# One addition moved from a DMA to VectorE, and single PSUM tiles at three places of a two-layer trunk

## The chip, the cores and the metric

The kernel runs on one core of one Trainium2 chip. The metric is the device time of one execution in microseconds, as the median of several. Before the change it is 2025.73 us, the median of three runs (2024.69 to 2026.8).

## What is computed

A trunk of two layers on x, 256 tokens by 2048 features, in float32. Layer 0 mixes by causal pooling, layer 1 by dilated attention over one shared K and V; each is followed by a norm, a gated FFN with a causal convolution of width 3, and another norm. Cut to what matters here:

```python
for i in range(DEPTH):                      # DEPTH = 2
    if i < N_A_LAYERS:                      # layer 0: w_in, pooling over 2/4/8/16 tokens, w_grp, w_out
        mix = pool_mixer(h, ...)
    else:                                   # layer 1: 16 heads of 128, three dilated windows merged
        mix = dilated_attention(h, k_shared, v_shared, w_q, w_o)
    h = layer_norm(DEEPNORM_ALPHA * h + mix, ln1_g[i], ln1_b[i])
    ff = conv_ffn(h, w_up, conv_w, conv_b, w_down)      # (silu(gate) * val) @ w_down
    h = layer_norm(DEEPNORM_ALPHA * h + ff, ln2_g[i], ln2_b[i])
```

## The kernel before

**Split products.** TensorE multiplies in a format that rounds float32. So each matrix is split into a high part (`wh`, `xc` high) and the rest (`wl`, `xc` low), and three products make one. ScalarE casts the high part, VectorE subtracts it for the low part: L99 and L100 for weights, L553 and L554 for x. Weights go through in *units* of 512 rows by 512 columns (1 MB). `run_units` works through a list of units in a fixed order: loads run up to five units ahead, splits up to three, and `later(n, fn)` puts a step n units on. `before[i]` holds steps for the start of unit i. Each engine's queue has the order in which this program writes its instructions; nothing is reordered.

**Activations.** The stream stands feature by feature in four quarters of 512 features, `H[0]` to `H[3]`, each 128 partitions by 4 blocks by 256 tokens. `XC[q]` is its split copy. At the start `x_quad(q)` turns a quarter of x by eight transposes (L548) into PSUM, casts and subtracts two halves of it into `XC[q]`, and later copies it into `H[q]` (L557). Quarters 1 to 3 are turned in the middle of units 0 to 2; a unit's first eight steps (blocks k = 0 and 1) lie ahead of them, the rest behind.

**PSUM.** One pool has four slots of two banks. `pair` takes a slot, and `bank` takes a slot too but uses only its first bank. The framework that places the waits goes by tile: a reader waits for all writers of a tile that stand ahead of it, and readers of one tile on two engines wait for each other. A new tile in a slot waits until the old one is read.

**Norms.** The residual of a group of four blocks is added to its quarter by VectorE (`resid_last`, L338 and L340). After quarter 0, its mean over features is made by a product with ones and turned round (`cs`, `shift`), and taken from all four quarters, so that the sums of squares stay small. The pooling layer and the attention do that with VectorE. In the first FFN (`first` is false) quarter 0 is done by VectorE (L394), and quarters 1 to 3 by DMAs from POOL's queue that add in place (`less`, L409). Then `stats` and `folds` gather sums S and squares Q over the quarters, and `chain` makes two products with ones of them (L429 and L430), behind the unit that follows the last quarter.

**The last two heads.** `outputs(3, (2, 3))` multiplies the weights of the attention with V for two heads into one PSUM tile (L1114, L1115), casts and subtracts each into `oq[3]` (L1119, L1120). It stands right ahead of the unit that reads them, the last of the first group of `attn_w_o`.

**The final norm.** `finish1` ends the second half of the tokens. Three quarters get b minus the mean times g from TensorE (L940 and L947), and VectorE multiplies the stream in from PSUM (L952, L955) ahead of the stores.

Of the kernel before, what the change touches and what calls it, by code (L numbers as in the profile page):

```python
# [9 lines left out]
F32 = mybir.dt.float32  # L10
# [3 lines left out]
OP = mybir.AluOpType  # L14
# [3 lines left out]
T = 256  # L18
P = 128
# [13 lines left out]
def trunk(ctx: ExitStack, tc: tile.TileContext, x, pool_w_in, pool_w_grp, pool_scale, pool_w_out,  # L33
# [3 lines left out]
    V, A, PE = nc.vector, nc.scalar, nc.tensor  # L37
# [10 lines left out]
    def pair(nm):  # L48
        return psp.tile([P, 2, 512], F32, name=nm, tag="ps")

    def bank(nm):
        return pair(nm)[:, 0, :]
# [19 lines left out]
    pending, before = [], {}  # L72
# [62 lines left out]
    def later(n, fn):  # L135
        if n == 0:
            fn()
        else:
            pending.append([n, fn])
# [158 lines left out]
    def w4(nm):  # L298
        return lnp.tile([P, 4, T], F32, name=nm, tag="w4")

    def quad_tile(nm):
        return xcp.tile([P, 4, 2, XW], F32R, name=nm, tag="xc")
# [12 lines left out]
    H, XC, XP, ST = {}, {}, {}, {}  # L315
    vec, cvec, gbx = [], [], {}
    ident = const.tile([P, P], F32, name="ident")
# [39 lines left out]
    def square(q, m):  # L357
        if m == 0:
            ST["sq"] = lnp.tile([P, 4, T], F32, name="sq", tag="sq")
        A.activation(ST["sq"][:, m:m + 2], H[q][:, m:m + 2], AF.Square)  # L360
# [12 lines left out]
    def folds(q):  # L373
        ST["S"] = fold(H[q], ST["S"], "S")
        ST["Q"] = fold(ST["sq"], ST["Q"], "Q")

    def stats(q):
        square(q, 0)
        square(q, 2)
        folds(q)  # L380

    def shift(s, first, lay, which):
        ps = bank("shift")
        PE.matmul(ps[:, :T], ones4, s, start=True, stop=True)
        if first:
            cs = ST["w4"][:, 3:4, :]
        else:
            cs = pools["ffn"].tile([P, 2, T], F32, name="cs", tag="xs", bufs=1)[:, 0:1, :]
        A.activation(cs[:, 0, :], ps[:, :T], AF.Copy, scale=-1.0)
        cb = cs.to_broadcast([P, 4, T])  # L390
        ST["S"] = ST["Q"] = None

        def one():
            V.tensor_tensor(H[0], H[0], cb, OP.add)  # L394
            if first:
                pre(1)
            stats(0)

        def two():
            xp(0, lay, which)  # L400
            if first:
                pre(2)
                pre(3)

        def pre(q):
            V.scalar_tensor_tensor(H[q], H[q], ALPHA, cb, op0=OP.mult, op1=OP.add)

        def less(q):
            nc.gpsimd.dma_start(H[q], cb, accum_op=OP.add)  # L409

        later(1, one)
        later(2, two)
        if not first:
            for q in (1, 2, 3):
                less(q)

    def xp(q, lay, which):
# [118 lines left out]
    def x_quad(q, halves=(0, 1)):  # L536
        xin = XIN
        if halves[0] == 0:
            H[q] = hp.tile([P, 4, T], F32, name="h", tag="h")
            XC[q] = quad_tile("xc")  # L540
        if halves[0] == 0:
            ST["xT"] = pair("xT")
        both = ST["xT"]
        for half in halves:
            for kk in range(2):
                for t in range(2):
                    k = 2 * half + kk
                    PE.transpose(both[:, half, kk * T + t * P:kk * T + t * P + P], xin[q, t][:, k * P:(k + 1) * P],  # L548
                                 ident)
        for half in halves:  # L550
            pv2 = both[:, half, :].rearrange("p (k t) -> p k t", k=2)
            s = slice(2 * half, 2 * half + 2)
            A.copy(XC[q][:, s, 0, :T], pv2)  # L553
            V.tensor_tensor(XC[q][:, s, 1, :T], pv2, XC[q][:, s, 0, :T].bitcast(F32), OP.subtract)  # L554
        if halves[-1] == 1:
            before.setdefault(min(q + 1, 3), []).append(
                lambda: A.copy(H[q], both.rearrange("p b (k t) -> p (b k) t", k=2)))  # L557

    def add_in(g, mids=()):
        group(pool_w_in[0], rows4, 512 * g, 512, xsrcs, pool_post(g), mode="a" if g == 3 else "ab", mids=mids)  # L560
# [3 lines left out]

    marks = []
    add_in(3, mids=[lambda q=q: x_quad(q) for q in (1, 2, 3)])
    add_in(2)
    add_grp(3)
# [295 lines left out]
    def tm_post(lay, n, c):  # L864
        parts = [slice(0, 256), slice(256, 512)]
        first, last = n == 0, n == 3
# [66 lines left out]
        def finish1():  # L933
            mv = lnp.tile([P, 6], F32, name="mv", tag="mv", bufs=2)
            V.bn_aggr(mv[:, 0:2], ST["bn"][:, 1])
            z = [HT[cc][:, 1, :] for cc in range(4)]
            g, b = [ST["g"][:, cc, :] for cc in range(4)], [ST["b"][:, cc, :] for cc in range(4)]
            ps = [p[:, i, :] for p in (pair("gb"), pair("gb")) for i in range(2)]
            for cc in range(3):
                PE.matmul(ps[cc], ident, b[cc], start=True, stop=False)  # L940
            A.activation(mv[:, 2:3], mv[:, 1:2], AF.Sqrt, bias=epst)
            V.reciprocal(mv[:, 3:4], mv[:, 2:3])
            V.scalar_tensor_tensor(mv[:, 4:5], mv[:, 0:1], -1.0, mv[:, 3:4], op0=OP.mult, op1=OP.mult)
            dg = w4("dg")[:, 0, :P]
            V.tensor_scalar(dg, ident, mv[:, 4:5], None, op0=OP.mult)
            for cc in range(3):
                PE.matmul(ps[cc], dg, g[cc], start=False, stop=True)  # L947
            V.scalar_tensor_tensor(z[3], z[3], mv[:, 0:1], g[3], op0=OP.subtract, op1=OP.mult)
            V.scalar_tensor_tensor(z[3], z[3], mv[:, 3:4], b[3], op0=OP.mult, op1=OP.add)
            store(nc.scalar, 3, 1)  # L950
            for cc in range(2):
                V.scalar_tensor_tensor(z[cc], z[cc], mv[:, 3:4], ps[cc], op0=OP.mult, op1=OP.add)  # L952
                store((nc.sync, nc.scalar)[cc], cc, 1)
            for by, c in zip((nc.sync, nc.scalar), parts):
                V.scalar_tensor_tensor(z[2][:, c], z[2][:, c], mv[:, 3:4], ps[2][:, c], op0=OP.mult, op1=OP.add)  # L955
                store(by, 2, 1, c)
# [7 lines left out]
    qk, pr, oq, pT, vts = {}, {}, {}, {}, {}  # L964
# [140 lines left out]
    def outputs(hq, ms):  # L1105
        if ms[0] == 0:
            oq[hq] = quad_tile("o")
        vt = vts[hq]
        both = pair("o")
        for m in ms:  # L1110
            hd = slice(m * P, (m + 1) * P)
            ps = both[:, m % 2, :]
            t = pT.pop((hq, m))
            PE.matmul(ps[:, :T], vt[:, 0, hd], t[:, :T], start=True, stop=False)  # L1114
            PE.matmul(ps[:, P:T], vt[:, 1, hd], t[:, T:], start=False, stop=True)  # L1115
        o = oq[hq][:, ms[0]:ms[0] + 2]
        for at in (slice(0, 1), slice(1, 2)) if hq == 3 else (slice(0, 2),):
            hi = o[:, at, 0, :T]
            A.copy(hi, both[:, at, :T])  # L1119
            V.tensor_tensor(o[:, at, 1, :T], both[:, at, :T], hi.bitcast(F32), OP.subtract)  # L1120

    def v_group(hq):
        js = (0, 1, 2, 3)
# [18 lines left out]
    with tc.tile_pool(name="start", bufs=1) as stp:  # L1142
        one1 = stp.tile([P, P], F32, name="one1")
        for q in range(NQ):
            for t in range(2):
                XIN[q, t] = stp.tile([P, 512], F32, name=f"xin{q}{t}")
            halves = [slice(0, 256), slice(256, 512)] if q == 0 else [slice(0, 512)]
# [130 lines left out]
```

## Time and profile before

| what | value |
|---|---|
| median of three runs | 2025.73 us |
| the profiled execution | 2024.98 us |
| its span | 2023.2 us |
| TensorE busy (share of the span) | 2011.6 us (99%) |
| VectorE busy | 1728.5 us (85%) |
| ScalarE busy | 1269.2 us (63%) |
| POOL busy | 94.3 us (5%) |
| granted TensorE clock over the span | 0.999 |
| mean DMA rate | 202 GB/s |

The span is what the profile sees of the execution; the rest of the 2024.98 us lies around it. TensorE's busy time counts overlapping products once, so a stop shows in the waits and in the timeline rather than in this share.

### The profile page before, as it was taken

The numbers are of one execution on the slowest core, as the hardware profiler recorded it, in microseconds if no ns is written. First come the engines' busy times: TensorE is split into PE (matmuls) and PEld (weight loads), VectorE is DVE, ScalarE is ACT, GpSimd is POOL, SyncE is SP. The second block draws the span as 40 slices with busy tenths as digits, with TensorE's granted clock in tenths as the row PEclk, the third lists the DMA queues.
The fourth block names the chain that finished last, engine by engine and source line by source line (L and its number), as shares of the span: only waits on it lengthen the run. The fifth ranks groups of instructions, "written<-read, shape, count | busy, mean of one in ns | idle before, by whom it ended". The sixth has DMA issues, their size and how long they took to land.

```text
span 2023.2 us, 31428 instructions
## 1 busy us (share of the span) xinstructions
PE 2011.6 (99%) x12742; PEld 1813.7 (90%) x12742; DVE 1728.5 (85%) x1822; ACT 1269.2 (63%) x1546; POOL 94.3 (5%) x154
## 2 busy tenths in 40 slices
PE   9999999999999999999999999999999999999999
PEld 8898988999899988888898988998899989989987
DVE  6868887999899999779796878787899899989898
ACT  5454686766766676656554444477767677667672
POOL 2000000000000000000000021000000000000000
PEclk9999999999999999999999999999999999999999
DMA  8565576676666767885565656557666757666765
GB/s 256 192 211 188 164 216 191 180 221 222 197 198 205 233 190 219 236 226 187 177 207 165 199 175 207 188 175 221 167 215 203 227 179 227 193 222 189 211 220 173
DMA packets 271825, 408.30 MB, mean 202 GB/s; under 512 B 74446, under 2 KB 86116, under 8 KB 271424
## 3 DMA queue, kind: packets, MB, share of 16 engines
q1 hardware_dynamic: 259488, 388.93, 59.1%
q0 software_dynamic: 11760, 16.70, 5.5%
q8 instruction: 100, 1.64, 0.3%
q10 hardware_dynamic: 432, 0.66, 0.1%
q14 instruction: 45, 0.37, 0.1%
HBM read 380.01 MB, written 2.10 MB: 189 GB/s over the span
## 4 chain that ended last, share of the span: by engine, by line
PE 98%; DVE 1%; DMA 0%; issue 0%; ACT 0%; SPq 0%; DVEq 0%
PE acc L180 44%; PE acc L181 22%; PE s L246 3%; PE s L244 3%; PE s L245 3%; PE acc L185 3%; PE t L246 2%; PE t L244 2%; PE t L245 2%; PE acc L184 2%; PE acc L183 2%; PE t L255 2%; PE t L257 2%; PE t L256 2%; PE s L1064 0%; PE o L1114 0%
## 5 line engine op out<-in xcount | busy, mean ns | idle before, releaser
L180 PE MATMUL acc<-xc,wh 128*128 128x512 f32 x3264 | 1151.8, 396 | 0.0
L181 PE MATMUL acc<-xc,wl 128*128 128x256 f32 x3264 | 916.0, 281 | 0.0
L100 DVE TENSOR_TENSOR wl<-raw,wh 128x2048 fp32r<-128x2048 f32 (+2 forms) x305 | 657.1, 2163 | 174.9 <-ACT wh L99 170.3
L180 PEld LDWEIGHTS acc<-xc,wh 128*128 128x128 f32 x3264 | 616.0, 189 | 143.3
L99 ACT CAST wh<-raw 128x2048 fp32r<-128x2048 f32 (+2 forms) x305 | 548.7, 1805 | 170.1 <-PE acc L180 70.4
L181 PEld LDWEIGHTS acc<-xc,wl 128*128 128x128 f32 x3264 | 615.4, 189 | 0.1
L113 ACT CAST wh<-raw 128x1024 fp32r<-128x1024 f32 x142 | 148.4, 1052 | 194.5 <-DVE raw L122 175.3
L114 DVE TENSOR_TENSOR wl<-raw,wh 128x1024 fp32r<-128x1024 f32 x142 | 169.4, 1221 | 11.2 <-ACT wh L113 11.2
L121 DVE TENSOR_TENSOR wl<-raw,wh 128x1536 fp32r<-128x1536 f32 x71 | 124.5, 1754 | 6.7 <-ACT wh L119 5.7
L119 ACT CAST wh<-raw 128x1536 fp32r<-128x1536 f32 x71 | 104.9, 1477 | 35.4 <-PE acc L180 28.2
L287 POOL DMA_DIRECT2D ht<-w x48 | 41.3, 1014 | 1446.7 <-DVE ht L877 722.1
L246 PE MATMUL t<-wh,g 128*128 128x256 f32 x376 | 105.7, 281 | 0.0
L244 PE MATMUL t<-wh,g 128*128 128x256 f32 x376 | 105.6, 281 | 0.0
L245 PE MATMUL t<-wl,g 128*128 128x256 f32 x376 | 105.4, 280 | 0.0
L620 ACT ACTIVATE c<-u,cv 128x256 f32<-128x256 f32 x172 | 89.5, 592 | 23.1 <-DVE f L682 16.6
L246 PE MATMUL s<-wh,xs 128*128 128x256 f32 x344 | 96.2, 280 | 0.0
L244 PE MATMUL s<-wh,xs 128*128 128x256 f32 x344 | 96.1, 279 | 0.0
L245 PE MATMUL s<-wl,xs 128*128 128x256 f32 x344 | 96.0, 279 | 0.0
L124 DVE TENSOR_TENSOR raw<-raw 128x1024 f32<-128x1024 f32 x71 | 87.0, 1225 | 2.4
L625 ACT ACTIVATE a<-u,cv 128x256 f32<-128x256 f32 x172 | 73.4, 499 | 11.9 <-DVE g L692 11.9
L611 ACT COPY u<-acc 128x512 f32<-128x512 f32 x84 | 46.9, 573 | 47.4 <-PE acc L181 47.1
L625 ACT ACTIVATE u<-u,cv 128x256 f32<-128x256 f32 x172 | 73.4, 499 | 0.0
(337 smaller groups left out, 3445.2 us busy)
## 6 DMA issues: line engine op xcount, KB each, us to landing
raw<-in_ffn_w_up_dram SPq DMA_DIRECT2D x160, 1024.0 KB, 5.2
raw<-in_ffn_w_down_dram SPq DMA_DIRECT2D x80, 1024.0 KB, 5.2
raw<-in_pool_w_out_dram SPq DMA_DIRECT2D x16, 1024.0 KB, 5.0
raw<-in_shared_w_k_dram SPq DMA_DIRECT2D x16, 1024.0 KB, 5.1
raw<-in_attn_w_q_dram SPq DMA_DIRECT2D x16, 1024.0 KB, 5.1
raw<-in_shared_w_v_dram SPq DMA_DIRECT2D x16, 1024.0 KB, 5.2
raw<-in_attn_w_o_dram SPq DMA_DIRECT2D x16, 1024.0 KB, 5.4
ht<-w POOLq DMA_DIRECT2D x50, 256.0 KB, 5.3
```

What stands on the lines that cost most here:

```text
L99: A.copy(wh[i][:, s], r[:, s])
L100: V.tensor_tensor(wl[i][:, s], r[:, s], wh[i][:, s].bitcast(F32), OP.subtract)
L113: A.copy(h[:, :, n], r[:, :, n])
L114: V.tensor_tensor(l[:, :, n], r[:, :, n], h[:, :, n].bitcast(F32), OP.subtract)
L119: A.copy(hs, rs)
L121: V.tensor_tensor(ls, rs, hs.bitcast(F32), OP.subtract)
L180: PE.matmul(ps[m].ap, h[:, k, c], q[:, k, :, :T], start=st, stop=False)
L181: PE.matmul(ps[m][:, :T], l[:, k, c], q[:, k, 0, :T], start=False, stop=sp)
L244: PE.matmul(to, xh, h[:, k, n], start=opens and kk == 0, stop=False)
L245: PE.matmul(to, xh, l[:, k, n], start=False, stop=False)
L246: PE.matmul(to, xl, h[:, k, n], start=False, stop=ends and kk == 1)
L625: A.activation(to[:, m, :], u[:, m, i:i + T], AF.Copy, scale=cv[:, i, j:j + 1])
```

## The change

Four edits.

1. In the first FFN the mean is added to quarter 1 by VectorE, right behind quarter 0, in the step `one`. Only quarters 2 and 3 are left to the DMAs.
2. `x_quad` takes a PSUM tile for each half of a quarter. The four transposes of a half are followed by its cast and its subtraction, then the next half's come. The copy into `H[q]` is made half by half, at the start of unit q instead of unit q + 1 (unit 3 for the last two quarters).
3. The last two heads get a PSUM tile each, and each head is cast and subtracted behind its own products. Heads 0 and 1 of that group are cast as one again.
4. The final norm's three products get a PSUM tile each instead of two tiles for pairs.

```diff
@@ shift, one()
             V.tensor_tensor(H[0], H[0], cb, OP.add)
             if first:
                 pre(1)
+            else:
+                V.tensor_tensor(H[1], H[1], cb, OP.add)
             stats(0)
...
         if not first:
-            for q in (1, 2, 3):
+            for q in (2, 3):
                 less(q)
@@ x_quad
-        if halves[0] == 0:
-            ST["xT"] = pair("xT")
-        both = ST["xT"]
         for half in halves:
+            ps = bank("xT")
             for kk in range(2):
                 for t in range(2):
                     k = 2 * half + kk
-                    PE.transpose(both[:, half, kk * T + t * P:kk * T + t * P + P], xin[q, t][:, k * P:(k + 1) * P],
-                                 ident)
-        for half in halves:
-            pv2 = both[:, half, :].rearrange("p (k t) -> p k t", k=2)
+                    PE.transpose(ps[:, kk * T + t * P:kk * T + t * P + P], xin[q, t][:, k * P:(k + 1) * P], ident)
+            pv2 = ps.rearrange("p (k t) -> p k t", k=2)
             s = slice(2 * half, 2 * half + 2)
             A.copy(XC[q][:, s, 0, :T], pv2)
             V.tensor_tensor(XC[q][:, s, 1, :T], pv2, XC[q][:, s, 0, :T].bitcast(F32), OP.subtract)
-        if halves[-1] == 1:
-            before.setdefault(min(q + 1, 3), []).append(
-                lambda: A.copy(H[q], both.rearrange("p b (k t) -> p (b k) t", k=2)))
+            before.setdefault(q, []).append(lambda s=s, pv2=pv2: A.copy(H[q][:, s, :], pv2))
@@ finish1
-            ps = [p[:, i, :] for p in (pair("gb"), pair("gb")) for i in range(2)]
+            ps = [bank("gb") for cc in range(3)]
@@ outputs
-        both = pair("o")
+        last = hq == 3 and ms[0] == 2
+        both = None if last else pair("o")
         for m in ms:
             hd = slice(m * P, (m + 1) * P)
-            ps = both[:, m % 2, :]
+            ps = bank("o") if last else both[:, m % 2, :]
...
+            if last:
+                hi = oq[hq][:, m, 0, :T]
+                A.copy(hi, ps[:, :T])
+                V.tensor_tensor(oq[hq][:, m, 1, :T], ps[:, :T], hi.bitcast(F32), OP.subtract)
-        o = oq[hq][:, ms[0]:ms[0] + 2]
-        for at in (slice(0, 1), slice(1, 2)) if hq == 3 else (slice(0, 2),):
-            hi = o[:, at, 0, :T]
-            A.copy(hi, both[:, at, :T])
-            V.tensor_tensor(o[:, at, 1, :T], both[:, at, :T], hi.bitcast(F32), OP.subtract)
+        if not last:
+            o = oq[hq][:, ms[0]:ms[0] + 2]
+            A.copy(o[:, :, 0, :T], both[:, :, :T])
+            V.tensor_tensor(o[:, :, 1, :T], both[:, :, :T], o[:, :, 0, :T].bitcast(F32), OP.subtract)
```

How the instructions stand on VectorE in the first FFN's norm, before. Each row has the line, the operation, what is written and read, and the size; `h_7393` is quarter 0 and `h_7713` quarter 1 of the stream, `cs` the mean turned round.

```order
L394 TENSOR_TENSOR h_7393<-h_7393,cs_8470 128x1024
L364 TENSOR_TENSOR fold_8426<-h_7393 128x512
L367 TENSOR_TENSOR S_8510<-fold_8426 128x256
L364 TENSOR_TENSOR fold_8426<-sq_8506 128x512
L367 TENSOR_TENSOR Q_8513<-fold_8426 128x256
L338 TENSOR_TENSOR h_7713<-h_7713,acc_8358 128x512
```

And on VectorE at the same place after the change, where `h_7401` is quarter 0 and `h_7721` quarter 1:

```order
L394 TENSOR_TENSOR h_7401<-h_7401,cs_8478 128x1024
L398 TENSOR_TENSOR h_7721<-h_7721,cs_8478 128x1024
L364 TENSOR_TENSOR fold_8434<-h_7401 128x512
L367 TENSOR_TENSOR S_8518<-fold_8434 128x256
L364 TENSOR_TENSOR fold_8434<-sq_8514 128x512
L367 TENSOR_TENSOR Q_8521<-fold_8434 128x256
L338 TENSOR_TENSOR h_7721<-h_7721,acc_8366 128x512
```

The addition onto quarter 1 now stands on VectorE directly behind that of quarter 0, ahead of the folds; the residual onto quarter 1 (L338) no longer has a DMA ahead of it.

ScalarE at the start, before. `xT_154` is the PSUM tile of quarter 0 and `xT_217` that of quarter 1, `xc` the split copies, `wh0` to `wh2` the weights of units 0 to 2, `h` the stream:

```order
L553 CAST xc_153<-xT_154 128x2x256
L99 CAST wh0_173<-raw0_93 128x512
L553 CAST xc_153<-xT_154 128x2x256
L99 CAST wh0_173<-raw0_93 128x512 x3
L553 CAST xc_216<-xT_217 128x2x256 x2
L99 CAST wh1_256<-raw1_115 128x512 x4
L557 COPY h_152<-xT_154 128x1024
L553 CAST xc_292<-xT_293 128x2x256 x2
```

ScalarE at the start after the change, where `xT_154` and `xT_177` are the halves of quarter 0, `xT_220` and `xT_227` those of quarter 1:

```order
L551 CAST xc_153<-xT_154 128x2x256
L99 CAST wh0_173<-raw0_93 128x512
L551 CAST xc_153<-xT_177 128x2x256
L99 CAST wh0_173<-raw0_93 128x512 x3
L553 COPY h_152<-xT_154 128x512
L553 COPY h_152<-xT_177 128x512
L551 CAST xc_219<-xT_220 128x2x256
L551 CAST xc_219<-xT_227 128x2x256
L99 CAST wh1_260<-raw1_115 128x512 x4
L553 COPY h_218<-xT_220 128x512
L553 COPY h_218<-xT_227 128x512
```

The copies of a quarter into the stream stand one unit earlier, ahead of the next quarter's casts, in two halves; the two casts of a quarter now read two tiles.

## The prediction

> **What bounds the kernel now.** I read the page first, then the waits of TensorE, then the timeline at each place where TensorE waits. The page:
>
> ```profile
> span 2023.2 us, 31428 instructions
> ...
> PE 2011.6 (99%) x12742; PEld 1813.7 (90%) x12742; DVE 1728.5 (85%) x1822; ACT 1269.2 (63%) x1546; POOL 94.3 (5%) x154
> ```
>
> TensorE (PE) is the bound, without gaps over nearly all of the span. An edit elsewhere pays only where TensorE stands still. The view of TensorE's waits (waiter, line, releaser: total us, times, longest) is short:
>
> ```profile
> PE acc L429 <- DVE S L370: 2.6, 1, 2.6
> ...
> PE acc L185 <- DVE wl L100: 0.9, 3, 0.3
> PE acc L430 <- DVE Q L370: 0.8, 1, 0.8
> PE xT L548 <- DVE xc L554: 0.5, 1, 0.5
> PE acc L180 <- DVE o L1120: 0.5, 2, 0.2
> ```
>
> All of these touch the change (the row left out is the warm-up of TensorE's first microsecond): L429 and L430 are the sums of the first FFN's norm, which the moved addition feeds; L185 and L548 stand where x is brought in; L180 waits for the last heads' outputs. The fourth place, the final norm, is the tail: there TensorE is done and the end waits for VectorE (DVE).
>
> **Part 1, the mean onto the second quarter (forecast 5.0 us).** The timeline of VectorE (start us, us, engine, line, operation, count, [idle before and its releaser]):
>
> ```profile
> 893.01 1.22 DVE L394 TENSOR_TENSOR h<-h,cs 128x1024 f32<-128x1024 f32 x1
> ...
> 896.32 0.43 DVE L367 TENSOR_TENSOR Q<-fold 128x256 f32<-128x256 f32 x1
> 901.48 0.69 DVE L338 TENSOR_TENSOR h<-h,acc 128x512 f32<-128x512 f32 x1 [4.73 <-DMA h<-cs]
> ...
> 930.28 1.28 DVE L338 TENSOR_TENSOR h<-h,acc 128x512 f32<-128x512 f32 x2
> ...
> 934.30 0.43 DVE L370 TENSOR_TENSOR Q<-Q,fold 128x256 f32<-128x256 f32 x1
> ```
>
> and the view of line L409, the issue of these additions on POOL's queue:
>
> ```profile
> L409 POOL DMA_DIRECT2D h<-cs x3: 1287/1701/2135, 890.2 to 892.0; - x3
> ...
> DMA to landing us min/median/max: 11.2/13.5/15.2
> ```
>
> VectorE reaches quarter 1's residual at 896.75 and stands until 901.48 for the DMA that adds the mean: issued at 890.2, plus 11.2, is 901.4. Now VectorE adds it itself. The row to price it by is its twin on quarter 0 (L394, same shape): 1.22 us. So L338 starts at 896.75 + 1.22 = 898.0 instead of 901.5. Removed: 4.73 of idleness, one DMA issue ahead of the other two on POOL's queue, 512 KB of traffic. Added: 1.22 of work ahead of quarter 0's folds. Net 3.5 earlier; I take 3.45.
>
> Does that arrive at Q (934.30)? Each step needs its input early enough. The two DMAs that are left land by 892.0 + 15.2 = 907.2 even if they get no faster, and the third quarter's residual is only due at about 911. The tightest is the cast of a weight that waits for TensorE:
>
> ```profile
> 904.96 1.49 ACT L99 CAST wh<-raw 128x1536 fp32r<-128x1536 f32 x1 [3.72 <-PE acc L180]
> ```
>
> It ends at 906.45, and VectorE would come for it at about 906.6: just in time. For quarter 3, TensorE's products end near 924.7 (48 products of 0.12 before 930.5, below) and VectorE now comes at 930.28 - 3.45 = 926.8. So Q ends at 934.73 - 3.45 = 931.28. TensorE there:
>
> ```profile
> 930.02 0.28 PE L185 MATMUL acc<-xp,wl 128*128 128x258 f32 x1
> ...
> 930.38 0.28 PE L185 MATMUL acc<-xp,wl 128*128 128x258 f32 x1
> 933.27 0.70 PE L429 MATMUL acc<-S,onesd 128*128 128x256 f32 x2 [2.61 <-DVE S L370]
> 934.78 1.22 PE L430 MATMUL acc<-Q,onesd 128*128 128x256 f32 x2 [0.82 <-DVE Q L370]
> 935.45 0.78 PE L183 MATMUL acc<-xp,wh 128*128 128x258 f32 x1
> ...
> 954.18 0.39 PE L180 MATMUL acc<-xc,wh 128*128 128x512 f32 x1
> ```
>
> Three products per 0.36 us (930.02 to 930.38) is 0.12 each, so L429 could have gone at 930.5. S now comes at 929.8, no wait; Q at 931.3, a wait of 0.3; L430 to the next product takes 0.67 here, I take 0.45 at the full clock. L183 then starts at about 931.8 instead of 935.45: 3.65 us. And the clock, in the busy times by stretch:
>
> ```profile
> 935.00:940.00 5.00, 5.00 (x28) 4.82 (x29) 4.42 (x7) 3.51 (x5) 0.00 (x0) 0.68 0.06 6
> ```
>
> The granted clock is the third figure from the end: after the stop TensorE gets 0.68 of its clock over these 5 us. From 935.45 to 954.18 lie 144 products, 17.3 us at 0.12, and they took 18.7: 1.4 us more, gone with the stop. Together 5.05. What is late next is the first product that reads XC (954.18), whose low part VectorE writes:
>
> ```profile
> 951.29 1.22 DVE L305 TENSOR_TENSOR xc<-h,xc 128x1024 fp32r<-128x1024 f32 x1
> ```
>
> It ends at 952.51, after the change at 949.06; TensorE would arrive at 954.18 - 5.05 = 949.13. The margin falls from 1.7 to about 0.1, so hardly more than 5.05 is to be had. I take 5.0, from 2.5 to 5.1; if VectorE was held by something else, -1.5.
>
> Should half of the stop stay (the first rival below), these rows give half of the 5.05, 2.5 us. [...]
>
> **Part 2, halves of x (forecast 2.2 us).** Before, both halves of a quarter stand in one PSUM tile. First the row of the weight loads' (PEld) waits in the first 46 us, then rows of the timelines of ScalarE, VectorE and TensorE by time:
>
> ```profile
> PEld acc L185 <- DVE wl L100: 2.0, 6, 0.6
> ...
> 7.97 1.98 ACT L99 CAST wh<-raw 128x512 fp32r<-128x512 f32 x3 [0.31 <-DMA raw<-in_pool_w_in_dram]
> 11.64 0.98 PE L548 MATMUL xT<-ident,xin 128*128 128x128 f32 x7 [0.37 <-DMA xin<-in_x_dram]
> 12.66 0.59 ACT L553 CAST xc<-xT 128x512 fp32r<-128x512 f32 x1 [2.71 <-PE xT L548]
> 14.01 0.59 ACT L553 CAST xc<-xT 128x512 fp32r<-128x512 f32 x1 [0.76 <-DVE xc L554]
> 15.23 2.49 DVE L100 TENSOR_TENSOR wl<-raw,wh 128x512 fp32r<-128x512 f32 x4
> 15.97 0.39 PE L185 MATMUL acc<-xc,wl 128*128 128x256 f32 x1 [0.29 <-DVE wl L100]
> ...
> 29.66 0.28 PE L184 MATMUL acc<-xc,wh 128*128 128x256 f32 x1
> ...
> 32.30 0.28 PE L183 MATMUL acc<-xc,wh 128*128 128x256 f32 x1
> ```
>
> ScalarE (ACT) starts only after all eight transposes (12.62), and its second cast waits for VectorE's subtraction of the first half. With a tile per half it starts after four, at about 12.1, casts both halves back to back to 13.3, and VectorE (subtraction 0.69 each) reaches the weight's low part at about 14.2 instead of 15.23: 1.0 earlier, where the longest single wait is 0.6. Weight loads wait 2.0 us in six places (first row); the issue times show a little more: 29.66 to 32.30 is 2.64 for 11 products of 0.12, 1.3 lost in unit 3 alone. By that measure the three units lose 2.4; I take 2.2, since in unit 3 VectorE needs 0.62 a piece against TensorE's 0.36 and 0.2 may stay. The first wait for VectorE (L548, 0.5) also goes, but brings nothing: the next transposes stand for x's own DMA until 11.64.
>
> The copies of x into H become two of about 0.59 (the cast of that shape) and move ahead of the next quarter's casts. Quarter 0's run from 9.95, when the weight casts end, to 11.1; the next quarter's halves take over their PSUM slots, the second at about 12.1. In units 1 and 2 they stand likewise between the weight casts and the next transposes; in unit 3 two halves are left where two whole quarters stood. The cover is ScalarE's idleness (2.71); if it were gone, up to 1.2 us a quarter. Bounds: -1 to 2.5.
>
> **Part 3, the last two heads (0.85 us).**
>
> ```profile
> 1234.77 0.37 ACT L1119 CAST o<-o 128x256 fp32r<-128x256 f32 x1 [2.64 <-PE o L1115]
> ...
> 1234.92 0.39 PE L180 MATMUL acc<-o,wh 128*128 128x512 f32 x1
> 1235.15 0.28 PE L181 MATMUL acc<-o,wl 128*128 128x256 f32 x1
> 1235.66 0.50 PE L180 MATMUL acc<-o,wh 128*128 128x512 f32 x1 [0.23 <-DVE o L1120]
> ...
> 1236.52 0.50 PE L180 MATMUL acc<-o,wh 128*128 128x512 f32 x1 [0.24 <-DVE o L1120]
> ```
>
> A pair of products takes 0.35 (0.23 + 0.12), so the steps 1234.92, 1235.66, 1236.52 lose 0.39 and 0.51. With its own tile the first head is cast while TensorE makes the second, and the second's chain loses the wait for VectorE (its cast at 1234.77, 0.8 later the product at 1235.66, which is when it is due). Gain 0.85; from 0.4 to 0.9.
>
> **Part 4, the final norm (0.45 us).**
>
> ```profile
> 2015.57 2.84 PE L947 MATMUL gb<-g,dg 128*128 128x512 f32 x6
> ...
> 2017.59 1.41 DVE L952 SCALAR_TENSOR_TENSOR ht<-ht,mv,gb 128x512 f32<-128x512 f32 x2 [0.63 <-PE gb L947]
> 2018.91 0.87 DVE L955 SCALAR_TENSOR_TENSOR ht<-ht,mv,gb 128x256 f32<-128x256 f32 x2
> ```
>
> Three products (two rows each) run to 2018.41. Product 0 is done at 2016.5, but VectorE waits 0.63 for product 1 in the same tile. Now it goes on at once and is held only by product 2, 2018.45 instead of 2018.91. From 0 to 0.5.
>
> **Sum.** 5.0 + 2.2 + 0.85 + 0.45 = 8.5 us. The profiled run took 2024.98 us, its span and 1.8 around it, 0.75 below the median of the runs shown. 2024.98 - 8.5 = 2016.5; against the median, 2017.2. Each gain stays to the end: what follows is paced by TensorE, and what it waits for moves with it.
>
> **Rivals.**
> - The wait changes its cause (0.15). VectorE is let go 3.5 us earlier but meets the weight cast or the next DMA, and half of TensorE's stop stays. For: the margin at that cast is 0.15 us. Against: it would have to slip by more than a microsecond. Part 1 gives 2.5: 2019.7.
> - Part 2 is held by the loads (0.08): x's and the weights' pieces come at the rate of the DMAs, and a shorter chain waits for them. For: the first unit waits for x until 11.64. Against: VectorE's four pieces from 15.23 follow each other without idling, so the loads were there. Part 2 gives 0.5: 2018.9.
> - The DMA is not what held VectorE (0.05). Then L338 still starts at 901.5, and the 1.22 us come on top: part 1 costs 1.5, the rest gives 3.5, in all 2.0: 2023.7, within the noise. The row's releaser and 890.2 + 11.2 speak against it. [...] The trace shows 11.2 at the least.
> - Slower (0.03): the three single tiles each take a slot of two banks, four slots in all, and every later group opens in another slot than before. If an opening product meets a tile that is still being read, it stands. Price: at 64 products to a group 51 groups open on L180 alone; at 0.3 us, under half a read (L338, 0.69), that is 15 us: 2025.7 - 8.5 + 15 = 2032. It decides where a slot's last read ends after TensorE arrives; the list of waits has no such entry now.
>
> Forecast 0.69, rivals 0.15, 0.08, 0.05, 0.03. A difference under 0.2% (4 us) is about what a measurement here cannot tell from none. Faster by more: 0.69 + 0.15 + 0.08 = 0.92, taken down to 0.91; within: 0.05 and the rest, 0.06; slower 0.03. The range reaches from all terms at their top with a fast run (9.0, and 1.0 for the spread of the runs shown) to the first two rivals with small terms low: 2015.6 to 2020.8.
>
> **What would show it.** Part 1: L338 near 898 without a wait for h<-cs, L429 without one, the clock at 1.00 after it. Part 2: no wait of L185 on L100 before 33 us, and no transpose that waits for a copy into H. Part 3: no wait on o. Part 4: VectorE's first product of the tail near 2017 less the shift. Wrong: L429 still waiting over a microsecond, or new waits at the groups' first products.

## The result and the profile after

The changed kernel takes 2016.63 us in the median of six runs (2016.33 to 2018.38), beside 2025.97 us for the kernel before in the same session (six runs, 2024.69 to 2026.80). The ratio is 0.9956, 95% interval 0.9943 to 0.9969. A second session gave 2016.24 beside 2024.95, ratio 0.9957 (0.9945 to 0.9970). The profiled execution of the changed kernel took 2016.33 us, 8.65 under that of before; its span is 2014.6. The forecast was 2017.2.

The page, and the list of TensorE's waits (waiter, line, releaser: total us, times, longest):

```profile
span 2014.6 us, 31425 instructions
...
PE 2008.5 (100%) x12742; PEld 1811.9 (90%) x12742; DVE 1729.0 (86%) x1822; ACT 1269.1 (63%) x1549; POOL 92.9 (5%) x153
```

```profile
PE warm L1163 <- DVE one L1159: 1.1, 1, 1.1
PE xT L548 <- DMA xin<-in_x_dram: 0.8, 1, 0.8
```

The list has no row more than these two: the waits for S, for Q, for the low parts of the first weights and for the heads are all gone. VectorE at the norm, its timeline after:

```profile
890.75 1.22 DVE L394 TENSOR_TENSOR h<-h,cs 128x1024 f32<-128x1024 f32 x1
891.89 1.22 DVE L398 TENSOR_TENSOR h<-h,cs 128x1024 f32<-128x1024 f32 x1
...
895.41 0.68 DVE L338 TENSOR_TENSOR h<-h,acc 128x512 f32<-128x512 f32 x1
...
928.42 0.43 DVE L370 TENSOR_TENSOR Q<-Q,fold 128x256 f32<-128x256 f32 x1
```

And TensorE's:

```profile
34.30 0.40 PE L180 MATMUL acc<-xc,wh 128*128 128x512 f32 x1
...
928.13 0.28 PE L185 MATMUL acc<-xp,wl 128*128 128x258 f32 x1
928.25 0.60 PE L431 MATMUL acc<-S,onesd 128*128 128x256 f32 x2
928.90 0.70 PE L432 MATMUL acc<-Q,onesd 128*128 128x256 f32 x2
929.25 0.47 PE L183 MATMUL acc<-xp,wh 128*128 128x258 f32 x1
...
946.77 0.48 PE L180 MATMUL acc<-xc,wh 128*128 128x512 f32 x1
```

L338 follows the fold without a bracket, so without waiting, and Q ends at 928.85, just ahead of the product that reads it (928.90). Set beside the rows of before, the same instructions give the gain place by place:

| TensorE or VectorE at | before | after | gained since the row above | forecast |
|---|---|---|---|---|
| first product of 512 columns (L180) | 36.56 | 34.30 | 2.26 | 2.2 |
| last product ahead of the norm's (L185) | 930.38 | 928.13 | -0.01 | 0 |
| first product behind them (L183) | 935.45 | 929.25 | 3.95 | 3.65 |
| first product that reads XC (L180) | 954.18 | 946.77 | 1.21 | 1.4 |
| first product on the last two heads | 1234.49 | 1227.41 | -0.33 | 0 |
| the fifth such product | 1236.97 | 1229.03 | 0.86 | 0.85 |
| final norm's products on g | 2015.57 | 2007.63 | 0.00 | 0 |
| VectorE's last products | 2018.91 | 2010.51 | 0.46 | 0.45 |
| end of the span | 2023.2 | 2014.6 | 0.2 | 0 |

The sum is 8.6 us, where the forecast had 8.5. The fifth row is a loss that the prediction did not have.

At the start of the program ScalarE's two casts of a quarter now follow each other, where the second waited 0.76 us for VectorE, and VectorE comes to the low parts of the weights at 14.01 instead of 15.23:

```profile
12.19 1.07 ACT L551 CAST xc<-xT 128x512 fp32r<-128x512 f32 x2 [0.91 <-PE xT L548]
14.01 2.49 DVE L100 TENSOR_TENSOR wl<-raw,wh 128x512 fp32r<-128x512 f32 x4
```

From TensorE's first product behind the transposes of quarter 1 to the same behind those of quarter 2, and from there to quarter 3, it takes 6.58 us where it took 7.11 before. From the last of these to the first product of 512 columns it takes 8.80 where it took 9.96. That is 0.53, 0.53 and 1.16 of the 2.26.

The last two places, TensorE behind the heads and VectorE at the end:

```profile
1227.84 0.39 PE L180 MATMUL acc<-o,wh 128*128 128x512 f32 x1
...
1228.19 0.40 PE L180 MATMUL acc<-o,wh 128*128 128x512 f32 x1
...
1228.57 0.50 PE L180 MATMUL acc<-o,wh 128*128 128x512 f32 x1
```

```profile
2008.94 1.46 DVE L948 SCALAR_TENSOR_TENSOR ht<-ht,mv,gb 128x512 f32<-128x512 f32 x2
2010.51 0.87 DVE L951 SCALAR_TENSOR_TENSOR ht<-ht,mv,gb 128x256 f32<-128x256 f32 x2
```

The steps of the products on the heads are 0.35 and 0.38 where they were 0.74 and 0.86, and VectorE's first product from PSUM has no wait of 0.63 any more.

### The profile page after: what moved, and what is told of

Same layout as the page of the kernel before. It is cut to its first block, busy times and chain, and to the rows that moved or that the text cites. A ratio compares the mean times of both kernels' runs of the same rounds, so it can differ in the third digit from the quotient of the medians.

```text
span 2014.6 us, 31425 instructions
## 1 busy us (share of the span) xinstructions
PE 2008.5 (100%) x12742; PEld 1811.9 (90%) x12742; DVE 1729.0 (86%) x1822; ACT 1269.1 (63%) x1549; POOL 92.9 (5%) x153
## 4 chain that ended last, share of the span: by engine, by line
PE 99%; DVE 1%; DMA 0%; SPq 0%; issue 0%; DVEq 0%
PE acc L180 44%; PE acc L181 22%; PE s L246 3%; PE s L244 3%; PE s L245 3%; PE acc L184 3%; PE acc L185 3%; PE acc L183 3%; PE t L246 3%; PE t L244 2%; PE t L245 2%; PE t L255 2%; PE t L257 2%; PE t L256 2%; PE s L1060 0%; PE o L1111 0%
## 5 line engine op out<-in xcount | busy, mean ns | idle before, releaser
L180 PE MATMUL acc<-xc,wh 128*128 128x512 f32 x3264 | 1152.1, 396 | 0.0
L180 PEld LDWEIGHTS acc<-xc,wh 128*128 128x128 f32 x3264 | 616.0, 189 | 143.6 <-issue 0.3
```

The lines of the kernel that those rows point to most:

```text
L180: PE.matmul(ps[m].ap, h[:, k, c], q[:, k, :, :T], start=st, stop=False)
```

## The experiments

The times of one kernel spread by 1 to 7 us within a session, so the traces carry the argument, and the medians stand beside them. For the norm one figure is used throughout, the *passage*: from the last product ahead of the norm's two (930.38 before) to the first that reads XC (954.18 before). It is 23.80 us before and 18.64 after.

### The four edits by themselves

**The mean alone.** The kernel before with this:

```diff
             if first:
                 pre(1)
+            else:
+                V.tensor_tensor(H[1], H[1], cb, OP.add)
             stats(0)
@@
-            for q in (1, 2, 3):
+            for q in (2, 3):
                 less(q)
```

> The kernel before with edit 1 alone (VectorE adds the mean to quarter 1; x, heads and final norm as before). Theory (VectorE was held by the DMA, and the stop of TensorE hung on that): no wait of L338 on the DMA, no wait of TensorE at the two norm products, clock 1.00 over the 10 us after them, and the first products that read XC each 0.1 us late; span 4.8 to 5.1 us under that of before, that is about 2018.3 for a span of 2023.2, and nothing changed before 890 us or after the first FFN. Rival (the gain needs the earlier start that the x halves give, since the margin at the weight cast is only 0.15 us): half of the stop stays and the span falls by 2.5 us or less.

Measured: 2020.33 us (11 runs) beside 2024.07 for before (33 runs, 2021.51 to 2026.48), ratio 0.9984 (0.9975 to 0.9993); span of the profiled run 2018.4. TensorE's timeline:

```profile
930.44 0.28 PE L185 MATMUL acc<-xp,wl 128*128 128x258 f32 x1
930.56 0.60 PE L431 MATMUL acc<-S,onesd 128*128 128x256 f32 x2
931.23 0.70 PE L432 MATMUL acc<-Q,onesd 128*128 128x256 f32 x2
931.58 0.47 PE L183 MATMUL acc<-xp,wh 128*128 128x258 f32 x1
...
949.10 0.47 PE L180 MATMUL acc<-xc,wh 128*128 128x512 f32 x1
```

The start of the norm stands where it stood (930.44), both waits are gone, and the passage is 18.66. From the first product on XC to the heads it takes 280.61 us where it took 280.31, so 0.3 is given back, as in the change. The gain in the trace is the same with the old start: the two edits do not lean on each other. The medians differ by only 3.7 us. One reason may be that the kernel before does not always pay for the clock: in ten of the 33 executions of it beside this run the granted clock over the span is 1.000, and 3.4 us at half the clock (granted 0.50), as in its first trace, would show as 0.999 (an estimate: 1.7 of 2023 us). No such execution was traced.

**The halves of x alone** (the kernel before with the change's `x_quad`):

```diff
-            ST["xT"] = pair("xT")
-        both = ST["xT"]
         for half in halves:
+            ps = bank("xT")
...
-        if halves[-1] == 1:
-            before.setdefault(min(q + 1, 3), []).append(
-                lambda: A.copy(H[q], both.rearrange("p b (k t) -> p (b k) t", k=2)))
+            before.setdefault(q, []).append(lambda s=s, pv2=pv2: A.copy(H[q][:, s, :], pv2))
```

> The kernel before with edit 2 alone (a PSUM tile for each half of x). Theory (the wait of ScalarE's second cast for VectorE delayed the low parts of the weights): TensorE is 2.2 to 2.3 us earlier at its first product of 512 columns (36.56 us before), keeps that to the first FFN's norm, loses the same 3.4 us there as before, and the span falls by 2.2 to 2.3 us, to about 2021.0. Rival (the DMA that adds the mean, and not TensorE, sets the time at that norm): the DMA moves with its issue, so nothing should be lost; if it does not move, the span falls by nearly nothing.

Measured: 2021.94 us (11 runs, 2.1 under before), ratio 0.9989 (0.9980 to 0.9998); span of the profiled run 2022.0, not 2021.0. The first product of 512 columns starts at 34.75, 1.8 earlier. VectorE's and TensorE's timelines at the norm, and the busy times by stretch (the clock is the third figure from the end):

```profile
899.53 0.69 DVE L338 TENSOR_TENSOR h<-h,acc 128x512 f32<-128x512 f32 x1 [4.59 <-DMA h<-cs]
```

```profile
931.32 1.22 PE L429 MATMUL acc<-S,onesd 128*128 128x256 f32 x2 [2.47 <-DVE S L370]
```

```profile
930.00:931.00 1.00, 0.00 (x0) 0.00 (x0) 0.93 (x3) 1.00 (x4) 0.00 (x0) 1.00 0.90 281
931.00:932.00 1.00, 0.68 (x2) 0.50 (x2) 0.96 (x3) 1.00 (x5) 0.00 (x0) 0.57 1.06 414
937.00:938.00 1.00, 1.00 (x7) 1.00 (x6) 0.52 (x1) 1.00 (x2) 0.00 (x0) 0.52 0.36 27
938.00:939.00 1.00, 1.00 (x10) 1.00 (x10) 1.00 (x1) 1.00 (x1) 0.00 (x0) 1.00 0.64 233
```

The DMA moved with its issue (L338 2.0 earlier, still waiting 4.59), so the rival that it stands still is out. But the same kind of stop cost more here. The granted clock was 0.50 from about 931.1 (0.57 over that microsecond) to 938.0, 6.8 us, where it was so for about 3.4 before (934.8 to 938.2), and the passage is 24.41. That, and the first weights, for which TensorE stood 1.5 us at 8.3 in this run, make up the missing microsecond.

This run does not part the two halves of the edit, the tiles and the earlier copies. The rows of before speak for the tiles: its copy into H (L557, 16.57 to 17.58) is followed by 2.19 us in which ScalarE idles, while the second cast waits 0.76 us for VectorE.

**Heads and final norm alone** (the kernel before with the change's `outputs` and this in `finish1`):

```diff
-            ps = [p[:, i, :] for p in (pair("gb"), pair("gb")) for i in range(2)]
+            ps = [bank("gb") for cc in range(3)]
```

> The kernel before with edits 3 and 4 alone (tiles for the last two heads and for the final norm). Theory: the two waits of L180 on the heads' low parts go (0.86 us), the last product of VectorE starts 0.46 us earlier against TensorE's last product; span 1.3 us lower, about 2021.9. Rival (the new order of PSUM slots behind the heads costs the second layer time): less than 0.8 us, with waits of TensorE at the first products of groups after 1236 us.

Measured: 2023.36 us (11 runs, 0.7 under before), ratio 0.9998 (0.9989 to 1.0006), which the medians alone cannot tell from no change; span of the profiled run 2022.4. From the first to the fifth product on the heads it is 1.62 us (1235.14 to 1236.76) against 2.48 before, 0.86 less. From the fifth to the final norm it is 778.60 in both, so the new order of PSUM slots costs the second layer nothing. VectorE's last products stand 2.88 behind TensorE's, against 3.34, 0.46 less. Both terms are the forecast's. What is missing from 1.3 lies elsewhere in the trace: this run was 0.32 later at 36.88 and lost another 0.32 at the norm (passage 24.12).

**All three quarters by VectorE** (the changed kernel with):

```diff
-                V.tensor_tensor(H[1], H[1], cb, OP.add)
+                for q in (1, 2, 3):
+                    V.tensor_tensor(H[q], H[q], cb, OP.add)
@@
-        if not first:
-            for q in (2, 3):
-                less(q)
```

> The changed kernel with the mean added by VectorE to quarters 2 and 3 as well, all behind quarter 0, and no such DMA. Theory (VectorE has no slack left there: the sum of squares is ready 0.05 us before TensorE asks for it, and what reads XC is already paced by VectorE): the two additions of 1.22 us arrive in full; S is ready about 1.5 us and Q about 2.4 us late, TensorE stops by about 2.4 us in all and the products on XC come 2.4 us later; with half the loss of clock that the whole stop had (0.7 us) the span rises by 2.4 to 3.1 us over that of the change. Rival (the DMAs crowd out the loads of the weights, so taking 1 MB of them away pays): the time stays within 0.5 us of the change's, or falls.

Measured: 2019.40 us (11 runs), span of the profiled run 2016.8, which is 2.2 over the change's. TensorE's waits:

```profile
PE acc L429 <- DVE S L370: 1.1, 1, 1.1
...
PE acc L430 <- DVE Q L370: 0.8, 1, 0.8
```

The passage is 20.71, 2.1 more than the change's. The two additions (2.4 us) arrive nearly in full, without any loss of clock (1.00 from 930 to 945 us): the expected 2.4 to 3.1 was too much by that loss and by some 0.4 of the additions. So one quarter fits on VectorE and the other two do not.

### How long a stop costs the clock

Needless repeats of a VectorE addition between S and Q of the last quarter, so that TensorE stands once, for a chosen time (the changed kernel with n = 2, 4, 6):

```diff
-                folds(3)
+                ST["S"] = fold(H[3], ST["S"], "S")
+                if not first:
+                    for i in range(n):
+                        V.tensor_tensor(ST["w4"][:, 0:2, :], H[3][:, 0:2, :], H[3][:, 2:4, :], OP.add)
+                ST["Q"] = fold(ST["sq"], ST["Q"], "Q")
```

> The changed kernel with two needless repeats of a VectorE addition (128x512, about 0.6 us each) between the sums S and the squares Q of the last quarter, so that TensorE stands once, for about 1.2 us, ahead of the product on Q. Theory of the prediction (the loss of clock goes in proportion to the stop): clock of about 0.9 over the next 5 us, 0.4 us lost by it, and in all 1.6 us more than the change. Rival (the clock falls only after a stop of more than some 3 us): clock 1.00, and 1.2 us more than the change.

> As the kernel with two repeats, with four: TensorE stands for about 2.4 us. In proportion: 0.8 us lost by the clock, 3.2 us more than the change. By a threshold of some 3 us: clock 1.00 and 2.4 us more.

> As the kernel with two repeats, with six: TensorE stands for about 3.7 us. In proportion: 1.2 us lost by the clock, 4.9 us more than the change. By a threshold of some 3 us: the clock is halved for about 3 us, as before the change, 1.4 us lost, 5.1 us more; the step comes between this run and the one with four.

TensorE's wait and the busy times behind it, for n = 4 and then for n = 6:

```profile
PE acc L436 <- DVE Q L374: 3.0, 1, 3.0
```

```profile
930.00:935.00 5.00, 3.37 (x26) 3.32 (x27) 4.93 (x8) 1.67 (x2) 0.00 (x0) 1.00 0.00 0
935.00:940.00 5.00, 5.00 (x44) 5.00 (x43) 4.36 (x6) 2.31 (x2) 0.00 (x0) 1.00 0.60 210
```

```profile
PE acc L436 <- DVE Q L374: 4.5, 1, 4.5
```

```profile
930.00:935.00 5.00, 0.84 (x6) 0.43 (x4) 4.69 (x8) 1.83 (x2) 0.00 (x0) 0.80 0.18 70
935.00:940.00 5.00, 4.69 (x20) 4.51 (x21) 4.42 (x8) 2.26 (x4) 0.00 (x0) 0.52 0.00 0
```

A repeat took about 0.74 us, not 0.6, so the stops were 1.57, 3.02 and 4.48 us. The passages are 20.15, 21.60 and 25.07: over the change's 18.64 that is 1.51, 2.96 and 6.43. The stops of 1.6 and 3.0 us cost themselves and the clock stays at 1.00; at 4.5 it falls to 0.50 and the stop costs 2.0 us on top. In proportion it is not. The rival's threshold of some 3 us was its author's estimate: these three runs agree with it, but with the halves alone the clock fell 2.3 us into a stop. That 3.0 us cost no clock may be in part luck of timing, by the table of the last section. (Times of the one run each: 2018.67, 2019.04 and 2024.47 us, beside 2021.49 for the one run of before taken with them, its lowest time of all; the third also lost the clock once at the start, 0.50 from 12 to 14 us.)

### The addition itself

The changed kernel with the mean added nowhere to quarter 1:

```diff
-            else:
-                V.tensor_tensor(H[1], H[1], cb, OP.add)
             stats(0)
```

> The changed kernel without any addition of the mean to quarter 1 (that part of the computation is left out), so VectorE is 1.22 us freer than in the change. Theory (in the change TensorE no longer waits for the sums at all, and what is left is the low part of XC, which VectorE writes just too late): nothing is won at the two norm products, the first products that read XC of quarters 0, 1 and 2 no longer open late, and the time falls by 0.2 to 0.3 us. Rival (VectorE's addition still costs TensorE its 1.22 us): the time falls by about 1.2 us.

Measured: 2016.13 us (one run, in the session of the stops), span 2014.4, passage 18.64: nothing won at the norm. VectorE's timeline:

```profile
904.07 1.76 DVE L100 TENSOR_TENSOR wl<-raw,wh 128x1536 fp32r<-128x1536 f32 x1 [1.11 <-ACT wh L99]
```

The 1.22 us that were freed are spent here, waiting for ScalarE's cast of a weight, which itself waits 3.72 us for TensorE in this run too. From there on VectorE runs as in the change. So the addition is hidden. The second half of the theory failed: the late openings on XC stay (946.61 to the heads takes 280.62), as VectorE is no earlier there.

The step that could move them is the order on VectorE. The changed kernel with:

```diff
-            if q > 0:
-                later(1 + q, lambda q=q: lo(q - 1))
             later(1 + q, lambda q=q: affine(q))
             if q < 3:
                 later(1 + q, lambda q=q: norm(q + 1))
-        later(5, lambda: lo(3))
+            later(1 + q, lambda q=q: lo(q))
```

> The changed kernel with one step moved: in each norm that is made by this code, VectorE writes the low part of a quarter of XC right behind the next quarter's normalization, ahead of the next low part of a weight instead of behind it. Theory (in the change the first products of three units behind the first FFN's norm open 0.05 to 0.13 us late, because the low part of XC ends at 946.63, 952.36 and 958.09 us, just before them, while its inputs are there more than 3 us earlier): the late openings go, and from the first product that reads XC to the last two heads it takes 280.3 us as before the change instead of 280.6; span 0.3 us under the change. Rival (then the low part of the weight comes too late for the same products): the openings stay as late or get later, and the time stays or rises by up to 1 us.

Measured: 2016.48 us (5 runs, 2015.11 to 2016.78), beside 2016.24 for the change in that session (5 runs); span of the profiled run 2013.3. VectorE's and TensorE's timelines:

```profile
941.83 1.22 DVE L305 TENSOR_TENSOR xc<-h,xc 128x1024 fp32r<-128x1024 f32 x1
```

```profile
945.91 0.39 PE L180 MATMUL acc<-xc,wh 128*128 128x512 f32 x1
```

The low part of XC is ready 2.9 us ahead of its reader, the product takes 0.39 instead of 0.48, and from it to the heads it is 280.31 us. The 0.3 us are back in the trace, and are far too little for the medians to show. It is the best of the spans, but most of its 1.3 us under the change's first trace is a luckier start (33.46).

**The change again:**

> The changed kernel again, for the spread. If the gain is what the traces of the single edits add up to (4.8 at the norm, about 2.3 at x, 0.9 at the heads, 0.5 at the end), the median lies 8 to 9 us under that of before. If the start, where the first loads land by up to 2 us earlier or later from run to run, decides more than the edits, the difference lies outside 6 to 11 us. The first 512-column product starts between 34.0 and 35.0 us, and everything behind it takes the same time to 0.1 us as in the first profile.

Measured: 2016.24 us, 8.7 under before; the first 512-column product at 33.78, passage 18.64. It started a little earlier than expected, and from XC to the heads took 0.12 more than in the first trace.

### The DMA

The kernel before, first with a copy in place of the addition, so that three quarters of the stream are overwritten with the mean, then with one of the three DMAs, so that two quarters keep theirs:

```diff
-            nc.gpsimd.dma_start(H[q], cb, accum_op=OP.add)
+            nc.gpsimd.dma_start(H[q], cb)
```

> The kernel before, where the three DMAs write the mean over quarters 1 to 3 of the stream in place of adding it (that part of the computation is changed; the bytes and the places are the same). In the 20 us from 888 us of the kernel before, the additions' 1584 packets took 49.2% of 16 engines, 0.099 us for about 1 KB, the weights' 1186 packets 0.104 us for about 2 KB. If the addition in place makes a packet dear, the first one lands 5 to 8 us after its issue, VectorE waits under 1 us at L338, and TensorE's stop ahead of the norm's products falls from 5.1 us to 2 or less. If it is the queue and the weights' traffic beside it, it lands after 11 us as before, and VectorE waits 4.7 us.

```diff
-            for q in (1, 2, 3):
+            for q in (1,):
                 less(q)
```

> The kernel before with the mean added by DMA to quarter 1 only, and not at all to quarters 2 and 3 (that part of the computation is left out). If the three additions and the weights share the DMA engines, one of them needs a third of 157 engine-us, 3.3 us of all 16, and lands 4 to 7 us after its issue: VectorE does not wait at L338, TensorE's stop falls by about 4 us, the clock stays at 1.00 and the span falls by about 5 us. If one such DMA takes 11 us by itself, the wait of 4.7 us and the whole stop stay.

Measured with the copy: 2021.43 us (one run, beside 2024.95 for before in that session), span 2019.7. The issue line's landing times, VectorE at L338, and the packets of the 20 us from 888 us:

```profile
DMA to landing us min/median/max: 9.1/10.5/11.7
```

```profile
899.23 0.69 DVE L338 TENSOR_TENSOR h<-h,acc 128x512 f32<-128x512 f32 x1 [2.72 <-PE acc L181]
```

```profile
q1 hardware_dynamic: 1316, 2.62, 41.7%
q0 software_dynamic: 432, 1.57, 21.8%
```

With one DMA: 2026.93 us (one run), span 2025.2, and the same three:

```profile
DMA to landing us min/median/max: 11.3/11.3/11.3
```

```profile
901.47 0.69 DVE L338 TENSOR_TENSOR h<-h,acc 128x512 f32<-128x512 f32 x1 [4.84 <-DMA h<-cs]
```

```profile
q1 hardware_dynamic: 1096, 2.15, 37.0%
q0 software_dynamic: 528, 0.52, 16.3%
```

Both expectations missed. One DMA by itself lands no sooner than three (11.3 us against 11.2), so it does not wait for its two sisters. A copy has 21.8% of the engines' time where the additions had 49.2%, yet lands only 2.1 us sooner. (The row names TensorE as the releaser, whose product had long been done; 890.0 plus 9.1 is 899.1, so it was the DMA.) So the addition in place accounts for 2.1 of the 11.2 us in this pair of traces. Where the rest lies, the packets of the one DMA show. It is issued at 890.1, and none of its packets starts before 894.9; in these 4.8 us the weights' packets take 73.2% of the 16 engines. Its 528 packets then start from 894.9 to 901.1, beside the weights', and would fill all 16 engines for 3.3 us (16.3% of 20) if they were alone. That the 4.8 us too are owed to the weights is argued, not shown: no run took the weights away from beside it.

The copy shows half a stop, too. VectorE waits 2.0 less (2.72 against 4.73), TensorE still waits 0.6 and 0.8, the clock stays at 1.00, and the passage is 20.24 against 23.80. Taking 2.0 us off the wait brought 3.6 in this pair of traces.

## Why the prediction was right, step by step

- **Part 1** was forecast at 5.0 and gave 4.83 in the first pair of traces (3.95 + 1.21 - 0.33), and 4.84 alone. The mechanism is as told: L338 no longer waits, S and Q come in time, the clock stays. Two small errors cancel. The stop went altogether, where 0.3 for Q and 0.1 more at the restart had been left in it, because VectorE came to quarter 3's residual 0.17 earlier than worked out and the restart took 0.35. And the margin of 0.1 at XC was not enough. L305 ends at 946.63 and the product that reads it starts at 946.77, but the first products on the first three quarters of XC lose 0.08, 0.10 and 0.13, which the step "hardly more than 5.05 is to be had" had seen for the first quarter only; with the low part written earlier they lose nothing.
- **The clock's 1.4 us** is the term that is not a constant. The passage of four kernels with the old stop was 23.80, 24.12, 24.41 and 25.08 (with one DMA), against 18.64, 18.64 and 18.66 without. So part 1 is worth 4.8 to 6.1 after the 0.3 at XC in these traces, and the execution that the forecast read stands at their low end. Where the old kernel keeps its clock, about 3.1 is left (an estimate: 4.8 less the 1.7 that 3.4 us at a granted 0.50 lose). The medians of the whole change gave 9.3 and 8.7 where the traced sum is 8.6, but those of the single edits, 3.7, 2.1 and 0.7, give only 6.6 in their session, where the whole change was not run. So that the forecast hit to 0.6 us is partly luck: it took one execution's loss of clock for the rule. (By its own terms the low end of the range comes to 2015.7, not 2015.6, and the first rival with the small terms at their lowest to 2020.6, where it has 2020.8; nothing hangs on either.)
- **The price of the first rival failed.** The prediction halved the 5.05 to 2.5 for half a stop. With the copy about half the stop was gone (waits of 0.6 and 0.8 us against 2.6 and 0.8) and 3.6 came back, with the clock at 1.00; stops of 1.6 and 3.0 us cost no clock either. Half of the 3.65 and the whole of the clock's 1.4, together 3.2 (an estimate from the rows of before), would have been the better price. The place that the rival named was right: without the addition VectorE is caught by that very cast (904.07). In the change it passes there without waiting, but has nothing to spare.
- **Part 2** was forecast at 2.2 and gave 2.26. The single traces spread: five kernels with whole quarters start their first 512-column product at 36.33 to 36.88, eight with halves at 33.46 to 34.92, means 36.57 and 34.22 (a ninth, n = 6, lost the clock at the start: 36.31). So it is 2.35 with half a microsecond or more on either side. The mechanism is as told: the second cast waits no longer, VectorE is 1.2 earlier at the low parts (forecast 1.0), and of the weight loads' 2.0 us of waits for them none is left in the first trace. The copies into H cost nothing that shows: no transpose waits for one. Its rival, held by the loads, is out.
- **Parts 3 and 4** gave 0.86 and 0.46, as forecast, in the change and alone.
- **The DMA as the holder** is confirmed by the copy: landing 2.1 sooner, it shortened the wait at L338 by 2.0. Beside the loads of the weights the copy took 9.1 us from issue to landing, and one addition alone 11.3.
- **The slower rival** is out. From the first 512-column product to the norm it takes 893.82 before and 893.83 after, and from the heads to the final norm 778.60 in both: no group opens later for another slot.

## What to carry to other kernels

Where one engine is busy nearly throughout, add up its few waits and trace each to its end; then ask how close the next waiter stands, since here a margin worked out at 0.1 us turned into 0.3 lost over three groups. A stop of TensorE cost about its length here where the clock stayed at 1.00 (1.51 us for 1.57, 2.96 for 3.02), and 1.2 to 2.4 us more behind it in the traces where the clock fell to 0.50, so shortening a long stop can pay more than the time taken off it: with the copy 2.0 us less of waiting brought 3.6. Nearly the same waits (2.6 and 0.8 us before, 2.7 and 0.8 with one DMA) were followed by 3.4 us at 0.50 in one trace and 6.8 in the other, so one trace does not give the price. An addition in place by DMA cost the engines only its issue here (1.3 to 2.1 us of POOL), but took 11.2 us at the least to land, and the engine that needed it could do it in 1.22.

## What was not expected of the hardware

- Length alone does not decide whether a stop costs the clock. One unbroken stop of 3.0 us cost no clock (1.00), while with the halves alone it was down (0.50) 2.3 us after TensorE's last product (928.86 to 931.1). In these traces the granted clock changes only in steps of 3.413 us (before the change it is 0.50 at the norm for one such step): from its first rise to the drop at the norm it is 925.012 us before, with the halves and with heads and norm (271 such steps), 928.425 with one DMA (272), and 918.185 from the rise ahead of it with n = 6 (269). Counted in these steps, TensorE's busy time at the norm tells the traces apart:

  | kernel | emptiest step, or the one ahead of the drop | TensorE busy in it, us | in the next | clock behind it |
  |---|---|---|---|---|
  | one DMA | 930.65 to 934.06 | 0.70 | 2.70 | 0.50 for 2 steps |
  | before | 931.38 to 934.79 | 0.70 | 3.42 | 0.50 for 1 step |
  | heads and norm | 932.30 to 935.71 | 0.97 | 3.41 | 0.50 for 1 step |
  | halves alone | 927.73 to 931.14 | 1.12 | 2.93 | 0.50 for 2 steps |
  | n = 6 | 929.57 to 932.98 | 1.27 | 1.09 | 0.50 for 2 steps |
  | n = 4 | 927.07 to 930.49 | 1.54 | 2.27 | 1.00 |
  | copy | 930.37 to 933.79 | 2.02 | 3.41 | 1.00 |
  | all three quarters | 927.01 to 930.42 | 2.12 | 2.81 | 1.00 |
  | n = 2 | 927.09 to 930.50 | 2.53 | 2.73 | 1.00 |

  So at the norm the clock fell behind a step with at most 1.27 us of products in it and came back behind the first full one. The stop of 3.0 us lay across two steps, with 1.54 and 2.27 us of products; that this spared it is argued from the table, not shown. The border is not sharp by this count: behind 1.65 us at the start of the run with n = 6 the clock fell, behind 1.59 near the end of before it did not. The steps ahead of these falls are not idle: they have 0.70 to 1.65 us of products. No run shifted one and the same stop against the steps on purpose.
- In six of the fourteen traces TensorE does not wait for the first unit's first weights at all, in the other eight it stands 0.7 to 1.9 us for them, and no edit touches those loads. The clock's first rise lies at different times, too: at 5.6 us with one DMA, at 9.8 before, at 10.7 with heads and norm. The start of the 512-column products spreads by 1.5 us among the kernels with halves, more than parts 3 and 4 together, and what share the loads and the clock have in that is not shown.
